# Reordering the second layer of a two-layer decoder step, with part of the state updates put off to the output projection

## The chip, the cores and the metric

The kernel runs on one core of a Trainium2 chip. The metric is the device time of one launch in microseconds (us). Before the change the median of three runs is 906.81 us (906.51 to 907.01). The profile comes from one further execution, taken by the hardware profiler.

The engines are TensorE (PE; its weight loads are shown apart, as PEld), VectorE (DVE), ScalarE (ACT), GpSimd (POOL) and SyncE (SP). SP and POOL mostly issue transfers here. Matrix results land in PSUM, which has eight banks; everything else lives in SBUF.

## The reference

One inference step of a decoder of two layers, width 2048, for 256 prompt tokens and 8 single sample tokens, 264 columns in all. Cut to what matters:

```python
# layer 0: sliding-window attention, 24 query heads; layer 1: HGRN2 recurrence, 12 heads of 128
# both: 4 memory cross-attention heads, a SiLU gate, one output projection, post-LayerNorm
q, f, iv, mq, g = _split(jnp.einsum('btd,de->bte', h, w_in), HG_SPLITS)
fg = lb + (1.0 - lb) * jax.nn.sigmoid(f)
qh, kh, vh = jax.nn.silu(q), 1.0 - fg, iv
# per token and head: state = fg * state + outer(kh, vh);  o = qh @ state
o = o * lax.rsqrt(jnp.mean(jnp.square(o), -1, keepdims=True) + RMS_EPS) * norm_w
branch = jnp.concatenate([o, mem_o], -1) * jax.nn.silu(g)
y = _layer_norm(ALPHA * h + jnp.einsum('bte,ed->btd', branch, w_out), ln_w, ln_b)
```

The memory heads of the sample tokens read cached keys and values (`cache_mem_k`, `cache_mem_v`); those of the prompt read keys and values projected from `mem_prompt`. Every sample token has its own 128x128 state for each of the 12 recurrent heads; the new states are outputs. The kernel also returns caches and the states of the prompt.

## The kernel before

**The stream.** Nearly all work hangs on one list of units, each with a block of 128 x 2048 float32 numbers (1 MB) that SP loads from memory: 16 x 128 x 128 weights of one output block, or a cache block, or states. `Stream.run` (L105) walks the list. A block passes through a `raw` buffer (four of them); ScalarE (L97) writes its high float16 half and VectorE (L98) the low half into an `hl` buffer (four of them too); then the unit's function uses it on TensorE. A raw buffer is free once its block is split, except for units added with `whole=True`: those write into the raw block and hold it until the unit is done. Splitting runs up to three units ahead of the unit that is being written.

**A projection.** `proj` (L307) multiplies the sixteen 128x128 blocks with the 264 columns of `xhl`, in three passes for each (high by high, high by low, low by high; L303 to L305), so 48 matmuls, into one of two PSUM banks with the tag `pj`. In layer 0 the keys and values of `kv_unit` take both `pj` banks and two more; in `mv_unit`, the last units before layer 1, the memory values take both `pj` banks.

**Side work.** Attention and recurrence are generators in the queue `side`. `after` (L1278) runs after each unit and moves the front generator on by one step (`pump(1)`). `hg_side` (L1064) computes one pair of recurrent heads over the prompt in ten steps; `memp_side` (L603) one memory head in two. `later` and `due` hold work that is put off by one unit, such as `hv_rows` (L1041).

**Layer 1.** For each of the six pairs the list has two forget gates (`f_unit`, L983), two value blocks (`hv_unit`, L1023), and then for each head a query block (`hq_unit`, L1009), the head's half block of states (`state_unit`, L1197) and, for heads below 8 (`NG1`), the head's gate (`early_gate`, L1051). Then come the four memory queries, with the four memory heads as side work, the four key-cache blocks (`ck_unit`, whose last one runs the softmax `mems_soft`, L659), the four value-cache blocks (`cv_unit`), with the remaining gates between and behind them, and then sixteen output units (`out_unit`, L767).

**A state unit** computes the sample tokens' outputs of one head by small matmuls (L1222 to L1226), and then updates the head's eight states in the raw block: L1233 spreads the value rows by matmuls with the selection matrix `sel`, ScalarE multiplies by the forget gate (L1237), VectorE adds the outer product (L1238), POOL writes the block out (L1241).

**Output units** add the projection to the residual stream (`residual`, L745), which frees the `pj` bank, and gather sums for the normalisation. The last eight keep their split weights in buffers of their own (`hold`) and treat first 176 columns, then, in `finish_tokens` (L841), the other 88.

**Order.** The code is traced in this order, and a planner then orders the instructions of each engine by their place in the program and by its own estimate of times. `tc.issue_after(x)` puts instructions of the same engine behind instruction `x`.

Of the kernel before, what the change touches and what calls it, by code (L numbers as in the profile page):

```python
# [18 lines left out]
P = 128  # L19
NC = 16  # L20
# [13 lines left out]
NG1 = 8  # L34
# [12 lines left out]
LEVELS = (1, 2, 4, 8, 16, 32, 64)  # L47
NMASK = (len(LEVELS) - 1) * 64

# [8 lines left out]
class Stream:  # L58


    def __init__(self, nc, pool, nraw, nsplit):
        self.nc, self.pool = nc, pool
        self.nraw, self.nsplit = nraw, nsplit
        self.units = []
        self.raw = {}
        self.hl = {}

# [37 lines left out]
    def run(self, pump):  # L105
# [11 lines left out]
        for i in range(n):  # L117
# [8 lines left out]
            while free < prepped and (free <= i or self.units[free][5]):  # L126
                free += 1
# [7 lines left out]
def trunk_kernel(  # L135
# [75 lines left out]
    bias_s = pm.tile([P, 2, NQ], F32, name="bias_s")  # L211

# [94 lines left out]
    def proj(hl, src, n, name, cols=slice(None), tag="pj"):  # L307
        w = hl.rearrange("p s (c f) -> p s c f", c=NC)
        pt = bank(tag, 2, name)
# [75 lines left out]
    def q_unit(j):  # L385
        def fn(hl):
            load_bias(j)
            load_bias(j + 1)
            pt = proj(hl, xhl, T, f"q{j}")
# [326 lines left out]

    fin = {0: deque(), 1: deque()}
# [14 lines left out]
    def silu2(out, pt):  # L732
        nc.scalar.activation(out, pt, AF.Tanh, scale=0.5 * CP)
        nc.vector.scalar_tensor_tensor(out, out, 1.0, pt, op0=ALU.add, op1=ALU.mult)
# [10 lines left out]
    def residual(l, i, cols, n, pt):  # L745
        z = xres[:, i, cols]
        summed = nc.vector.scalar_tensor_tensor(z, z, ALPHA / CP, pt, op0=ALU.mult, op1=ALU.add)  # L747
# [235 lines left out]
    def f_unit(h):  # L983
        def fn(hl):
# [4 lines left out]
            pt = proj(hl, xhl, T, f"f{h}")  # L989
            i = h % 2  # L990
            if i == 0:
# [3 lines left out]
                cur["ks8"] = p1.tile([P, 2, TS], F32, tag="ks8", name=f"ks8{h}", bufs=2)  # L995
            fg, kk, ks8 = cur["fg"][:, i], cur["kk"][:, i], cur["ks8"][:, i]
# [6 lines left out]
            nc.vector.tensor_scalar_mul(ks8, kk, 1.0 / (SA * SK))  # L1003
# [5 lines left out]
    def hq_unit(h):  # L1009
        def fn(hl):  # L1010
# [5 lines left out]
            if h % 2 == 1:  # L1016
                side.append(hg_side(h // 2, cur["q"], cur["vn"], cur["fg"], cur["qk"]))
# [3 lines left out]
    later, due = [], []  # L1021

    def hv_unit(h):  # L1023
        def fn(hl):
# [3 lines left out]
            if i == 0:  # L1028
                cur["vn"] = p1.tile([P, 2, 2, P], F32, tag="vn", name=f"vn{h}", bufs=2)
                cur["vr"] = p1.tile([P, 2, P], F16, tag="vr", name=f"vr{h}", bufs=2)  # L1030
# [10 lines left out]
    def hv_rows(h, vt, vs, vn, vr):  # L1041
# [7 lines left out]
        nc.vector.tensor_copy(vr[:, i], p16)  # L1049
# [14 lines left out]
    def hg_side(pi, q, vn, fg, qk):  # L1064
# [119 lines left out]
        for i, sq in enumerate(sqs):  # L1184
# [3 lines left out]
            scaled = mix[:, h] if h >= NG1 else sq  # L1188
# [3 lines left out]
            if h < NG1:  # L1192
# [4 lines left out]
    def state_unit(h):  # L1197
        def fn(hl):
            p1 = H["p"]
            pi, i = h // 2, h % 2  # L1200
            raw = stream.raw[state_at[h]][:, : TS * P]
            R = raw.rearrange("p (b v) -> p b v", b=TS)
            v = hl[:, :, : TS * P].rearrange("p s (b v) -> p s b v", b=TS)
            vr, fgs, ks8 = cur["vr"][:, i], cur["fg"][:, i, TP:T], cur["ks8"][:, i]
# [228 lines left out]
```

## Time and profile before

| what | value |
|---|---|
| median of three runs | 906.81 us (906.51 to 907.01) |
| profiled execution | 906.08 us |
| its span, first to last instruction | 904.3 us |
| mean granted TensorE clock | 0.994 |
| TensorE matmuls | 9281 |
| DMA | 198.67 MB, mean 220 GB/s |

Matmuls are pipelined: a row's duration covers the whole way through the array, and the next matmul may start long before it ends. A TensorE that is shown as busy is therefore not idle, and may still wait a little; idle time is counted from the end of the last matmul. The share of busy time is an average over stages. By the timeline, layer 0 ends and the first forget gate of layer 1 starts at about 420 us, the output units of layer 1 at about 800 us, and their second columns at about 878 us.

### The profile page before, as it was taken

The numbers are of one execution on the slowest core, as the hardware profiler recorded it, in microseconds if no ns is written. First come the engines' busy times: TensorE is split into PE (matmuls) and PEld (weight loads), VectorE is DVE, ScalarE is ACT, GpSimd is POOL, SyncE is SP. The second block draws the span as 40 slices with busy tenths as digits, with TensorE's granted clock in tenths as the row PEclk, the third lists the DMA queues.
The fourth block names the chain that finished last, engine by engine and source line by source line (L and its number), as shares of the span: only waits on it lengthen the run. The fifth ranks groups of instructions, "written<-read, shape, count | busy, mean of one in ns | idle before, by whom it ended". The sixth has DMA issues, their size and how long they took to land.

```text
span 904.3 us, 21814 instructions
## 1 busy us (share of the span) xinstructions
PE 886.6 (98%) x9281; PEld 762.9 (84%) x9281; DVE 701.5 (78%) x1230; ACT 582.4 (64%) x982; POOL 34.9 (4%) x68
## 2 busy tenths in 40 slices
PE   9999999999999999999999999999999999799996
PEld 6888889678888888876888888898888888688996
DVE  6879877669886666697687887979788989678736
ACT  6767776657664444476766877777777585858415
POOL 1100010000000000002000000000000000000000
PEclk9999999999999999999999999999999999899999
DMA  9998566557785555556374655827454878456303
GB/s 340 392 353 317 188 245 209 188 208 265 262 333 192 187 192 203 207 198 214 127 292 137 216 201 174 299 101 260 160 215 164 303 283 308 172 207 244 130 2 97
DMA packets 37853, 198.67 MB, mean 220 GB/s; under 512 B 4555, under 2 KB 10732, under 8 KB 17532
## 3 DMA queue, kind: packets, MB, share of 16 engines
q1 hardware_dynamic: 33024, 181.55, 56.3%
q0 software_dynamic: 4688, 15.67, 4.6%
q8 instruction: 72, 1.18, 0.5%
q14 instruction: 25, 0.20, 0.1%
q10 hardware_dynamic: 44, 0.07, 0.0%
HBM read 180.03 MB, written 17.22 MB: 218 GB/s over the span
## 4 chain that ended last, share of the span: by engine, by line
PE 77%; DVE 8%; ACT 6%; DMA 6%; issue 3%; SPq 0%; ACTq 0%; DVEq 0%
PE o L303 5%; PE o L305 5%; PE o L304 5%; PE g L305 5%; PE g L303 5%; PE g L304 5%; DVE hl L98 4%; ACT hl L97 2%; PE hv L305 2%; PE hv L303 2%; PE hv L304 2%; DMA raw<-in_w_in 2%; PE hq L303 2%; PE hq L305 2%; PE hq L304 2%
## 5 line engine op out<-in xcount | busy, mean ns | idle before, releaser
L98 DVE SCALAR_TENSOR_TENSOR hl<-raw,hl 128x2048 f16<-128x2048 f32 (+2 forms) x168 | 358.6, 2138 | 82.0 <-ACT hl L97 81.0
L97 ACT ACTIVATE hl<-raw 128x2048 f16<-128x2048 f32 (+2 forms) x168 | 299.2, 1784 | 97.8 <-PE o L305 45.4
L305 PEld LDWEIGHTS <-hl 128*128 128x128 f16 (+2 forms) x2048 | 197.4, 98 | 31.8 <-DVE hl L98 2.9
L303 PEld LDWEIGHTS <-hl 128*128 128x128 f16 (+2 forms) x2048 | 197.3, 98 | 30.6 <-issue 2.2
L304 PEld LDWEIGHTS <-hl 128*128 128x128 f16 (+2 forms) x2048 | 197.4, 98 | 30.3 <-issue 2.2
L305 PE MATMUL g<-xhl,hl 128*128 128x264 f16 x512 | 142.0, 277 | 2.4 <-DVE hl L98 2.4
L303 PE MATMUL g<-xhl,hl 128*128 128x264 f16 x512 | 141.9, 277 | 0.0
L304 PE MATMUL g<-xhl,hl 128*128 128x264 f16 x512 | 141.9, 277 | 0.0
L303 PE MATMUL o<-mix,hl 128*128 128x264 f16 x384 | 105.4, 276 | 0.8 <-DVE xres L747 0.8
L304 PE MATMUL o<-mix,hl 128*128 128x264 f16 x384 | 105.8, 276 | 0.0
L305 PE MATMUL o<-mix,hl 128*128 128x264 f16 x384 | 105.7, 276 | 0.0
L303 PE MATMUL q<-xhl,hl 128*128 128x264 f16 x192 | 53.0, 276 | 1.0 <-DVE kst L251 1.0
L303 PE MATMUL f<-xhl,hl 128*128 128x264 f16 x192 | 52.9, 276 | 0.4 <-DVE mvhl L251 0.4
L305 PE MATMUL hv<-xhl,hl 128*128 128x264 f16 x192 | 53.0, 276 | 0.0
L303 PE MATMUL hq<-xhl,hl 128*128 128x264 f16 x192 | 53.0, 276 | 0.0
L304 PE MATMUL hq<-xhl,hl 128*128 128x264 f16 x192 | 53.0, 276 | 0.0
L305 PE MATMUL hq<-xhl,hl 128*128 128x264 f16 x192 | 53.0, 276 | 0.0
L304 PE MATMUL hv<-xhl,hl 128*128 128x264 f16 x192 | 53.0, 276 | 0.0
L303 PE MATMUL hv<-xhl,hl 128*128 128x264 f16 x192 | 53.0, 276 | 0.0
L304 PE MATMUL q<-xhl,hl 128*128 128x264 f16 x192 | 53.0, 276 | 0.0
L305 PE MATMUL q<-xhl,hl 128*128 128x264 f16 x192 | 53.0, 276 | 0.0
L304 PE MATMUL f<-xhl,hl 128*128 128x264 f16 x192 | 52.9, 276 | 0.0
(338 smaller groups left out, 1858.4 us busy)
## 6 DMA issues: line engine op xcount, KB each, us to landing
raw<-in_w_in SPq DMA_DIRECT2D x88, 1024.0 KB, 6.4
raw<-in_w_o SPq DMA_DIRECT2D x32, 1024.0 KB, 5.0
raw<-in_w_mk SPq DMA_DIRECT2D x8, 1024.0 KB, 4.9
raw<-in_w_mv SPq DMA_DIRECT2D x8, 1024.0 KB, 4.9
raw<-in_c_mk SPq DMA_DIRECT2D x8, 1024.0 KB, 5.1
raw<-in_c_mv SPq DMA_DIRECT2D x8, 1024.0 KB, 7.0
raw<-in_state SPq DMA_DIRECT2D x12, 512.0 KB, 5.4
out_ss<-raw POOLq DMA_DIRECT2D x12, 512.0 KB, 5.5
```

Of the source, the lines that this page charges most:

```text
L97: hi = self.nc.scalar.activation(hl[:, 0, s], raw[:, s], AF.Copy, scale=scale)
L98: lo = self.nc.vector.scalar_tensor_tensor(hl[:, 1, s], raw[:, s], scale, hl[:, 0, s], op0=ALU.mult, op1=ALU.subtract)
L303: mm(out, lhs(0), rhs(0), start=start, stop=False)
L304: mm(out, lhs(0), rhs(1), start=False, stop=False)
L305: return mm(out, lhs(1), rhs(0), start=False, stop=stop)
```

## The change

**Order of layer 1.** The list now begins with the first forget gate and the memory queries; the eight cache blocks stand one by one between projections of the first two pairs, with `q0` and `g0` between the last key block and the first value block. Every unit says how many side steps follow it (`pumps`: 0 behind caches and states, 2 behind many projections of the recurrence). Gates of heads 0, 1, 2, 4 and 6 (`EARLY`) stand within the pairs; eleven gates stand at the end. 

**State units.** One for each pair, with the whole 1 MB block; the small operations run once on both heads.

**Updates.** Heads 0 to 5 are updated at their pair, the second head one unit later (`later`); the raw block is held one unit longer (`longer`). For heads 6 to 11 (`LATER`) the value rows, forget gates and keys are written to memory (`kept`), and their raw block is free after the split. `fetch` reads the states and what was kept again, on POOL's queue, into buffers of the memory heads that are no longer used (three homes), first behind the seventh of the last gates. `with_update` updates one head behind the residual of output units 1, 3, 5, 7, 9 and 11, and fetches the head three later.

**Banks.** The first query of layer 0 and the first forget gate of layer 1 take the bank `pv`, and do all 32 passes with the high weights before the 16 with the low ones (`apart`).

**Scaling.** The factor of `ks8` moves into `sel`.

```diff
-NG1 = 8
+EARLY = (0, 1, 2, 4, 6)
+LATER = tuple(range(6, HD))
+KEPT = P // 2 + 2 * TS
...
-            while free < prepped and (free <= i or self.units[free][5]):
+            while free < prepped and (free + self.longer.get(free, 0) <= i or self.units[free][5]):
...
+    kept = {pi: dp.tile([P, 2, KEPT], F32, name=f"kept{pi}") for pi in sorted({h // 2 for h in LATER})}
...
+        if apart:
+            pt = bank("pv", 1, name)
+            for k, (c, s, r) in enumerate([(c, 0, r) for c in range(NC) for r in range(2)] + [(c, 1, 0) for c in range(NC)]):
+                mm(pt[:, :n], w[:, s, c], src[:, r, c, cols], start=k == 0, stop=k == 3 * NC - 1)
+            return pt[:, :n]
...
-            pt = proj(hl, xhl, T, f"q{j}")
+            pt = proj(hl, xhl, T, f"q{j}", apart=j == 0)
...
-            pt = proj(hl, xhl, T, f"f{h}")
+            pt = proj(hl, xhl, T, f"f{h}", apart=h == 0)
...
-            nc.vector.tensor_scalar_mul(ks8, kk, 1.0 / (SA * SK))
...
+    def update(h, R, vr, fgs, ks, sel):
+        for g in range(2):
+            pvb = bank("pt", 2, f"vb{h}{g}")
+            for bb in range(4):
+                mm(pvb[:, bb * P : (bb + 1) * P], sel[:, 4 * g + bb], vr, start=True, stop=True)
+            for bb in range(4):
+                b = 4 * g + bb
+                s = R[:, b]
+                nc.scalar.activation(s, s, AF.Copy, scale=fgs[:, b : b + 1])
+                nc.vector.scalar_tensor_tensor(
+                    s, pvb[:, bb * P : (bb + 1) * P], ks[:, b : b + 1], s, op0=ALU.mult, op1=ALU.add
+                )
+        nc.gpsimd.dma_start(ss_o[h // 2, :, h % 2 * TS * P : (h % 2 + 1) * TS * P], R.rearrange("p b v -> p (b v)"))
...
+    def fetch(h):
+        if not homes:
+            aside["sel"] = cp.tile([P, TS, P], F16, tag="ms", name="late_sel", bufs=2)
+            nc.gpsimd.dma_start(aside["sel"], sel_d)
+            aside["kept"] = cp.tile([P, len(LATER), KEPT], F32, tag="ms", name="late_kept", bufs=2)
...
+            for t in (mkhl, mvhl, mqhl):
...
+        homes.rotate(-1)
+        aside[h] = homes[-1]
+        nc.gpsimd.dma_start(aside[h], state[h // 2][:, (h % 2) * TS * P : (h % 2 + 1) * TS * P])
...
+    def with_update(fn, k):
+        def f(hl):
+            fn(hl)
+            with tc.issue_after(marks["o"].ins):
+                late_update(LATER[k])
+                if k + 3 < len(LATER):
+                    fetch(LATER[k + 3])
...
+            if 2 * pi in LATER:
+                tail = vr[:, :, P // 2 :]
+                nc.vector.tensor_copy(tail[:, :, :TS], fgs)
+                nc.vector.tensor_copy(tail[:, :, TS:], ks)
+                nc.gpsimd.dma_start(kept[pi], vr)
+                return
...
+            half(0)
+            later.append(lambda: half(1))
...
+    f_of(0)
+    for h in range(NM):
+        w1("mq", h, mem1_sides(mq_unit(h)) if h == NM - 1 else mq_unit(h))
+    cache(c_mk, ck_unit, 0)
+    f_of(1, 2)
+    cache(c_mk, ck_unit, 1)
+    v_of(0, 2)
+    cache(c_mk, ck_unit, 2)
+    v_of(1)
+    cache(c_mk, ck_unit, 3)
+    q_of(0)
+    gate_of(0)
+    cache(c_mv, cv_unit, 0)
+    gate_of(1)
+    cache(c_mv, cv_unit, 1)
+    q_of(1)
+    cache(c_mv, cv_unit, 2)
+    f_of(2, 2)
+    cache(c_mv, cv_unit, 3)
+    f_of(3, 2)
+    state_of(0)
...
+    for k, j in enumerate([j for j in range(NC) if j not in EARLY and j not in last] + list(last)):
+        w1("g", j, fetch_first(gate_unit(1, j)) if k == 6 else gate_unit(1, j))
...
-        pump(1)
+        pump(pumps.get(i, 1))
...
-        sel[b, b] = 1
-        sel[TS + b, b] = 1
+        sel[b, b] = 1 / (SA * SK)
+        sel[TS + b, b] = 1 / (SA * SK)
```

175 lines of the change are left out of this document (101 added, 74 removed).

## The prediction

> **What bounds the kernel now.** I read the page first, then the list of waits of TensorE, then a table of stretches, then the timeline at the places where TensorE waits.
>
> ```profile
> span 904.3 us, 21814 instructions
> PE 886.6 (98%) x9281; PEld 762.9 (84%) x9281; DVE 701.5 (78%) x1230; ACT 582.4 (64%) x982; POOL 34.9 (4%) x68
> ```
>
> TensorE is busy for 98% of the span. The arithmetic stays nearly the same, so a reordering can only win back idle time of TensorE and time at a reduced clock. The idle time, by what ended it:
>
> ```profile
> PE g L305 <- DVE hl L98: 2.4, 2, 1.7
> PE hpo L1169 <- ACT st L1147: 1.5, 1, 1.5
> ...
> PE q L303 <- DVE kst L251: 1.0, 1, 1.0
> PE mback L677 <- DVE mrows L674: 1.0, 1, 1.0
> PE o L303 <- DVE xres L747: 0.8, 2, 0.5
> PE f L303 <- DVE mvhl L251: 0.4, 1, 0.4
> PE msc L303 <- ACT osq L1183: 0.4, 1, 0.4
> PE hpo L1171 <- ACT s L1162: 0.3, 1, 0.3
> ```
>
> The stretches (columns: stretch, length, busy time of each engine with its count, granted clock, share of the DMA engines, GB/s) say where this lies:
>
> ```profile
> 420.00:700.00 280.00, 279.64 (x2947) 247.47 (x2947) 229.01 (x441) 204.80 (x372) 13.09 (x24) 1.00 0.57 199
> 700.00:740.00 40.00, 39.96 (x469) 35.61 (x467) 34.63 (x67) 27.09 (x33) 1.61 (x3) 1.00 0.76 277
> 740.00:762.00 22.00, 22.00 (x274) 19.47 (x273) 22.00 (x26) 15.03 (x15) 0.00 (x0) 1.00 0.89 322
> 762.00:800.00 38.00, 32.50 (x368) 26.91 (x366) 30.70 (x51) 26.93 (x47) 0.54 (x1) 0.91 0.61 228
> 800.00:847.00 47.00, 46.23 (x416) 40.14 (x415) 37.31 (x42) 32.12 (x32) 0.00 (x0) 1.00 0.60 221
> 847.00:878.00 31.00, 31.00 (x406) 30.82 (x405) 12.43 (x30) 3.75 (x11) 0.00 (x0) 1.00 0.01 2
> ```
>
> One jam stands out, 762 to 800 us: TensorE idles 38.00 - 32.50 = 5.5 us and runs at 0.91 of its clock. From 420 to 762 it idles 0.4 us in all. Just before the jam VectorE is busy 22.00 of 22.00 us: there the last pair of recurrent heads, the four memory heads, eight cache blocks and the gates all fall together. The timelines of TensorE and ScalarE show how it closes:
>
> ```profile
> 769.24 1.91 ACT L97 ACTIVATE hl<-raw 128x2048 f16<-128x2048 f32 x1 [3.84 <-issue]
> 775.73 0.28 PE L677 MATMUL mback<-ident,mrows 32*128 32x32 f32 x2 [0.99 <-DVE mrows L674]
> 777.00 0.17 PE L696 MATMUL mso<-msphl,hl 128*128 128x2 f16 x1
> ```
>
> The value-cache blocks (mso) are split early, but cannot be multiplied before the softmax of the key scores is back (mback, 775.73). Until then they sit in the four split buffers, ScalarE has nowhere to write a gate's weights (idle 3.84 us before 769.24), and the gates come late.
>
> **The change, part by part.**
>
> *Layer 1 in another order.* Cache blocks and memory heads go to the front, one cache block to each projection, before the first recurrent side work starts; between the last key block and the first value block stand two projections (q0, g0) where one gate stood. The last stretch keeps eleven gates and the last pair. What this can win is the whole jam: 5.5 us idle, 38 x (1 - 0.91) = 3.4 us of clock, and the refill after each wait. Idle is counted from the modelled end of a matmul (0.28 us), while matmuls follow each other every 0.11 us, so six waits (g twice, hpo twice, mback, msc) cost 6 x 0.17 = 1.0 us more. Together 9.9 us.
>
> By the Trainium skill, "TensorE: Matmul & The Clock Gate", Part 1, the clock is halved only after about 3.4 us without work. Here it fell though the longest wait on the list inside the stretch is 1.7 us, so the measured 0.91 decides; by the page's rule the dip had another cause, and 3.4 us of the 9.9 would stay.
>
> Does the work fit elsewhere? Rows of 420 to 800 us, VectorE and then ScalarE:
>
> ```profile
> L98 DVE SCALAR_TENSOR_TENSOR hl<-raw,hl 128x2048 f16<-128x2048 f32 x64 | 146.6, 2292 | 21.2 <-ACT hl L97 20.8
> L1238 DVE SCALAR_TENSOR_TENSOR raw<-vb,ks,raw 128x128 f32<-128x128 f32 x96 | 26.7, 345 | 0.2 <-PE vb L1233 0.2
> L98 DVE SCALAR_TENSOR_TENSOR hl<-raw,hl 128x1024 f16<-128x1024 f32 x12 | 14.7, 1222 | 1.8 <-ACT hl L97 1.7
> L1003 DVE TENSOR_SCALAR ks<-kk 128x8 f32<-128x8 f32 x12 | 2.2, 184 | 0.1
> L1227 DVE TENSOR_REDUCE qf<-hos 128x8 f32<-128x16 f32 x12 | 2.1, 171 | 1.8 <-PE hos L1226 1.8
> L1228 DVE TENSOR_TENSOR qk<-hos,hvt 128x8 f32<-128x8 f32 x12 | 1.9, 157 | 0.0
> L1237 ACT ACTIVATE raw<-raw,fg 128x128 f32<-128x128 f32 x96 | 29.5, 391 | 3.5 <-DVE hl L98 3.5
> ```
>
> VectorE is busy 229.01 + 34.63 + 22.00 + 30.70 = 316.3 of 380 us there. It loses half of the state updates (48 x 26.7/96 = 13.4), the twelve ks8 scalings (2.2), 14.7 - 6 x 2.29 = 1.0 by splitting six state blocks instead of twelve halves, and about 6.5 by doing the seven small operations of a state unit (1.9 to 2.1 us each in sum) six times instead of twelve. Six pairs of copies (under 0.2 us each) come back. About 295 remain for 370 us, 80%. A pair without one gate unit loses its cover of 5.4 us of TensorE (48 matmuls at 0.112) but also its split, 2.29 us of VectorE; the middle stays about as full as it is, and there it hardly waits today.
>
> The put-off half lands behind the residuals of output units 1, 3, 5, 7, 9 and 11. VectorE has 78 - 37.31 - 12.43 = 28 us free between 800 and 878, ScalarE 78 - 32.12 - 3.75 = 42; the updates bring 13.4 and 48 x 29.5/96 = 14.8. They fit in sum. The danger is order: a burst of eight (2.2 us) and a split (2.29) can stand before the next residual, which frees a projection bank. Eight-unit stretch by TensorE: 48 x 0.112 = 5.4 us a unit, no wait; the later units take 31.00/406 x 48 = 3.7 us, so 2.2 + 2.3 + 0.3 = 4.8 is 1.1 too long, at most at three or four of them. Bounds 0 to 4 us; I take 1.0, since VectorE has finished its splits early in this stage today (12.43 of 31 us from 847). Ending early also clears the tail: unit 11 lies four units before the end of the stage.
>
> *Transfers.* The fetches go to POOL's queue: 3 MB of state read again, three small writes and reads of what is kept, and the twelve write-outs, of which six move.
>
> ```profile
> raw<-in_state SPq DMA_DIRECT2D x12, 512.0 KB, 5.4
> out_ss<-raw POOLq DMA_DIRECT2D x12, 512.0 KB, 5.5
> ```
>
> The DMA engines are at 0.60 from 800 to 847 and 0.01 after, which hides them; uncovered, 3 MB would be some 14 us at 221 GB/s. Head k+3 may be fetched when head k is written out: 2.2 + 5.5 + 5.5 = 13 us, against six units between them (2 x 5.4 + 4 x 3.7 = 25.6 us at worst). POOL queues nothing urgent behind these waits; SP's weight loads are not behind them. On SP, six full state loads replace twelve half ones.
>
> By the Trainium skill, "SBUF — State Buffer", section "SBUF: two separate sides", a transfer issued from GpSimd can starve while VectorE runs certain two-port operations, which speaks against moving fetches to POOL. The rows do not show it: 5.5 us there against 5.4 on SP. By the page the fetches would come late, which is a rival below.
>
> *A bank of their own.* The first query waits for a bank that the key copies still read, the first forget gate for one that the memory values still fill:
>
> ```profile
> 29.22 0.28 PE L305 MATMUL kv<-xhl,hl 128*128 128x264 f16 x1
> 30.50 0.27 PE L303 MATMUL q<-xhl,hl 128*128 128x264 f16 x1 [1.00 <-DVE kst L251]
> ...
> 419.28 0.38 PE L593 MATMUL mv<-hl,mhl 128*128 128x512 f16 x1
> 420.09 0.27 PE L303 MATMUL f<-xhl,hl 128*128 128x264 f16 x1 [0.43 <-DVE mvhl L251]
> ```
>
> Start to start is 1.28 us against 0.11, and 0.81 against 0.22: 1.17 and 0.59 us. What is late next is q0's own split:
>
> ```profile
> 25.34 1.91 ACT L97 ACTIVATE hl<-raw 128x2048 f16<-128x2048 f32 x1 [2.71 <-DMA raw<-in_w_in]
> ...
> 27.28 2.29 DVE L98 SCALAR_TENSOR_TENSOR hl<-raw,hl 128x2048 f16<-128x2048 f32 x1 [2.77 <-ACT hl L97]
> ```
>
> The high half is there at 27.25, the low half at 29.57; with the 32 high passes first the low one is needed at 29.3 + 32 x 0.112 = 32.9. Both waits go; the arrival at later weights is 1.2 us earlier, and the next units have a larger lead. I take 1.0 + 0.5 (bounds 0 and 1.76).
>
> *Fewer matmuls.* The ones-products fall from 24 to 12:
>
> ```profile
> L1226 PE MATMUL hos<-qkh,ones 128*128 128x8 f16 x24 | 2.3, 166 | 0.0
> ```
>
> Half of 2.3 us is the upper bound; each 0.166 is mostly pipeline under its neighbours, so I take 0.3.
>
> **The sum.** 9.9 + 1.0 + 0.5 + 0.3 = 11.7 us off, and on: 1.0 in the output stage, and 1.0 for new small waits in layer 1 (0 to 3; 0.4 us today over 342 us). Net 9.7. The profiled execution took 906.1 us for a span of 904.3, so it would take 896.4; the median of the runs is 906.8, 0.7 above, so about **897.0**.
>
> **Rivals.**
>
> *The jam moves to the front.* The value-cache blocks now share their stretch with the first recurrent pair and the first state unit. If their softmax is late again, the same buffers clog, and up to the 9.9 us come back: 897 to 907, half of it (902) as a value. For: VectorE needs about 35 us there (nine splits, 20.6; one update, 2.2; two thirds of a pair's side work: what the rows above leave of 316.3 us is 112, under 19 a pair, so 12) for four projections (21.6), four cache blocks and side products, about 28 us of matmuls. Against: two projections instead of one cover the softmax, and splits stand ahead of side work.
>
> *The output stage pays.* VectorE's bursts delay residuals at every later unit: 4 us instead of 1.0, 900.
>
> *The clock stays low for another reason.* The stretch 762 to 800 is granted 0.91 while the longest wait is 1.7 us; if another cause holds it, 3.4 us remain: 900.4. Against it: every other stretch up to 878 has 1.00.
>
> *POOL's transfers come late.* An update that waits for its block stands in VectorE's queue before the next residual. It decides when write and fetch take over 25.6 - 2.2 = 23.4 us; at three times the 5.5 us row (33) head 11 is 9.6 us late: 907.
>
> *State blocks starve the weights (the slower side).* In pairs 0, 1 and 2 the raw buffer is now held until the second half, issued after the following unit, is written out. Today's chain of waits already runs through such a buffer:
>
> ```profile
> 515.43 1.38 DVE raw L1238 x5
> ...
> 519.78 7.85 DMA raw<-in_w_in
> ```
>
> If the second half runs where it is written and the fourth unit behind takes that buffer: state unit and next unit with its side work about 7.8 us, update 2.2, write 5.5, load 7.9, split 1.9 + 2.3 = 27.6 us, against three projections (16.2) with side products and the state unit, an estimated 20.4 us. That is 7.2 us of waiting three times, 21.6, and the total is 919. It decides from the point where the write-out lands later than 20.4 - 12.1 = 8.3 us after the state unit starts on TensorE. Against: today updates run long before their unit,
>
> ```profile
> 512.30 0.61 PE L1233 MATMUL vb<-vr,sel_t 128*128 128x128 f16 x8
> ...
> 521.68 0.17 PE L1222 MATMUL hos<-qfh,hl 128*128 128x2 f16 x1
> ```
>
> (9 us ahead here), and the other three buffers turn over meanwhile.
>
> **How the numbers follow.** The forecast gets 0.57. The front jam gets 0.16 (0.08 faster, 0.06 within, 0.02 slower), the output stage 0.08 (faster), the clock 0.03 (faster), POOL 0.02 (slower), starving 0.14 (0.01 faster, 0.01 within, 0.12 slower). A difference of 0.2%, 1.8 us, is about what a measurement of this kernel can tell from no change. So faster 0.77, same 0.07, slower 0.16. Everything won at no cost (9.9 + 1.76 + 0.3 + the 0.8 at o) gives 894.0; a little below is the low end, 893. The upper end takes in the output stage and nearly all of the front jam: 906.
>
> **What would show it.** Right: no stretch of layer 1 with TensorE idle over 1 us in 20, clock 1.00 there, VectorE below full for every 20 us, q and f gone from the list of waits, VectorE busier by some 13 us in the output stage with TensorE's wait for xres below 2 us. Wrong: a wait of g, f or hq for hl behind a state unit (starving), mback late again near the front, or o waiting for xres at most odd units.

## The result, and the profile after

The changed kernel takes **921.66 us** (919.22 to 921.84) where the kernel before takes 906.91 us (906.51 to 907.09) in the same session: a ratio of 1.0157 [1.0139, 1.0175]. The forecast was 897.0, range 893 to 906: wrong in sign, and outside the range. The kernel before was timed again beside each group of runs below, with medians of 905.79 to 906.55 us; every ratio is to the one of its own group.

The profiled execution took 921.59 us, its span 919.8. First TensorE's waits of the changed kernel (engine, line, what it waited for: us in all, times, longest):

```profile
PE hq L307 <- DVE vs L255: 4.8, 2, 2.9
PE o L307 <- ACT mix L739: 4.8, 1, 4.8
PE o L307 <- DVE xres L757: 4.3, 3, 2.5
PE hs L307 <- ACT qk L1088: 2.2, 3, 1.2
...
PE hpo L1178 <- ACT st L1156: 1.1, 1, 1.1
PE rms L1191 <- ACT osq L1186: 0.9, 1, 0.9
```

Of the waits of before, g for hl, q for kst, f for mvhl and mback are gone; hpo still waits a little for st and s, and o for xres 4.3 us where it was 0.8. New ones took the place of the rest. The table of stretches of the same kernel says where:

```profile
660.00:720.00 60.00, 51.87 (x514) 43.75 (x513) 38.53 (x73) 41.62 (x76) 3.26 (x6) 0.97 0.47 167
720.00:797.00 77.00, 77.00 (x808) 67.88 (x807) 64.05 (x104) 50.15 (x74) 1.63 (x3) 1.00 0.49 169
797.00:822.00 25.00, 18.36 (x167) 15.12 (x166) 10.70 (x19) 11.53 (x19) 0.54 (x1) 0.86 0.24 90
822.00:850.00 28.00, 28.00 (x259) 24.48 (x257) 26.64 (x39) 21.94 (x24) 2.15 (x4) 1.00 0.78 293
850.00:887.00 37.00, 32.73 (x408) 31.56 (x406) 25.13 (x62) 13.50 (x29) 2.67 (x5) 1.00 0.36 136
```

The old jam ahead of the output stage is quite gone (77.00 of 77). TensorE now idles 8.1 us at 660 to 720, 6.6 at 797 to 822 and 4.3 at 850 to 887. In the first two of these stretches VectorE is busy 38.53 of 60 us and 10.70 of 25, and ScalarE 41.62 and 11.53: TensorE waits although no other engine is full. So each engine waits for another in turn, and the question is what order makes them do so.

For the comparisons below I worked out of each trace what TensorE lost: the time from the start of one matmul to the start of the next, less the mean of that step for the same shape without a wait in the kernel before. That counts idle time and time at a reduced clock alike. The end of TensorE's work less this loss lies between 875.9 and 876.9 us in every run here, so the loss accounts for the differences. Each row is one profiled execution, and that is its grain: ahead of 420 us all kernels but `before` and `spread4_one_bank` run the same code, and still lose between 5.4 and 10.1 us there. The profiled execution of no_put_off, at 923.44 us, was also its slowest. A difference of one or two us in one cell shows little by itself. In us, by stretch:

```
                  0-420  420-640  640-720  720-800  800-830  830-end   sum
before              7.6      1.0      0.3     10.1      0.5      1.0  20.6
after               5.9      2.9     11.9      0.1      9.4      5.1  35.3
bank_alone          6.6      0.7      0.7     11.4      0.8      0.8  21.1
no_put_off         10.1      1.9     11.4      3.4     10.4      1.1  38.3
act_behind          5.9      2.2      9.7      1.7      2.6      1.3  23.4
raised200           6.5     17.4      1.2      3.9      5.6      3.5  38.0
first2              6.6      6.5      5.2      0.8      8.7      2.0  29.8
first1              5.8     13.0      0.4      0.6      9.0      0.9  29.7
mem_last            6.7      0.4      6.5     11.1      1.3      0.6  26.4
cv_last             6.5      1.3     11.6      6.6      2.0      1.3  29.2
caches_last         7.3      0.7     10.5     12.6      0.0      0.6  31.7
own_queue           5.4      6.4      4.8      1.0      2.0      1.3  20.8
spread4             5.5      2.0      2.1      2.7      0.2      1.3  13.8
spread5             6.4      1.5      1.9     10.5      0.0      0.4  20.7
spread4_no_put      6.1      2.0      9.2      3.8      9.0      1.1  31.1
spread4_hoist       6.3      1.6      4.1      1.9      2.0      5.1  20.8
spread4_one_bank    7.5      1.5      2.1      1.6      2.0      1.3  16.1
```

After less before: 10.0 won at 720 to 800 and 1.7 ahead of 420; 1.9, 11.6, 8.9 and 4.1 lost in the others. By the sums that is 14.7 us, by the medians 14.75.

**Two things are seen in the trace of after.** The first is on ScalarE, whose timeline has these rows (start, duration, line, operation, count, idle time before and what ended it):

```profile
671.42 1.86 ACT L1214 ACTIVATE mkhl<-mkhl,late_kept 128x128 f32<-128x128 f32 x6 [4.40 <-DMA late_kept<-kept]
673.30 1.28 ACT L1192 ACT_TABLE_LOAD   x1
...
718.66 0.48 ACT L1192 ACTIVATE osq<-rms,eps_rms 128x264 f32<-128x264 f32 x1 [0.98 <-PE rms L1191]
720.23 2.15 ACT L1214 ACTIVATE mqhl<-mqhl,late_kept 128x128 f32<-128x128 f32 x7 [1.09 <-DMA late_kept<-kept]
722.29 0.46 ACT L1192 ACTIVATE osq<-rms,eps_rms 128x264 f32<-128x264 f32 x1
...
856.38 2.45 ACT L1214 ACTIVATE mvhl<-mvhl,late_kept 128x128 f32<-128x128 f32 x8 [3.56 <-DMA mvhl<-in_state]
858.74 3.69 ACT L100 ACTIVATE held<-raw 128x2048 f16<-128x2048 f32 x2
```

L1214 scales a put-off head's states. Those of heads 6 to 8, meant for the output stage, run at 671 to 678 and 720 to 724 us, in the midst of the pairs. The line that puts the update off binds VectorE only: `issue_after` holds back the instructions of the engine of the one that it names. ScalarE takes its instructions in order, so it stands 4.40 us for a transfer with the logarithm and the exponential of a pair behind it. At the second place VectorE stands 7.95 us for such an exponential, as the first row here shows:

```profile
724.52 0.49 DVE L1198 SCALAR_TENSOR_TENSOR osq<-osb,small_t,osq 128x264 f32<-128x264 f32 x1 [7.95 <-ACT osq L1195]
...
860.67 2.29 DVE L101 SCALAR_TENSOR_TENSOR held<-raw,held 128x2048 f16<-128x2048 f32 x1 [3.36 <-ACT held L100]
```

The second row is the output stage: the block of head 10, fetched late (issue to landing 10.0 us in the median of the two `mvhl<-in_state`, against 5.4 for `raw<-in_state` before), stops ScalarE for 3.56 us in front of two splits of output weights; VectorE's half of the split and the residual behind it come late, and o waits 2.5 us.

The second thing is the recurrence of the prompt. Its ten steps are one chain a pair, and a pair can hardly begin before the one ahead of it is done: st, prod and kn have one buffer each. By the timeline (us; query: a pair's last query matmul ends; hd: its chain begins):

```
             query, pairs 0 to 5           hd, pairs 0 to 5              last rms   first o
before       459 512 565 618 664 702       459 512 565 618 669 730       777        799.9
after        497 535 583 630 682 729       489 564 620 675 721 775       812        797.5
first2       452 521 577 634 681 727       452 521 609 668 719 768       810        796.1
mem_last     452 503 547 594 639 686       452 511 570 626 674 715       768        805.2
own_queue    451 514 566 622 687 723       451 514 575 628 687 748       799        798.8
spread4      451 516 569 626 672 716       451 516 575 627 690 741       792        791.8
```

Before, the chain began with the queries until the last two pairs. A chain needs both heads of its pair, and those of pair 0 now stand apart: their hd start at 489 and 501 us, where before they started at 459 and 463. So the chain goes on 38 us later. The pairs follow each other in 38 to 52 us while the chain takes 46 to 63 a pair (hd to hd, pair 0 counted from 501): it is 29 to 46 us behind from the second pair on, and ends when the output units already run. ScalarE's timeline of after shows how that reaches TensorE:

```profile
660.82 0.38 ACT L1171 ACTIVATE s<-pu 128x256 f32<-128x256 f32 x1 [3.21 <-PE pu L1167]
...
662.05 1.91 ACT L100 ACTIVATE hl<-raw 128x2048 f16<-128x2048 f32 x1 [0.57 <-PE hv L309]
663.87 0.58 ACT L1182 ACTIVATE osb<-hpo 128x512 f32<-128x512 f32 x1
...
665.87 0.18 ACT L253 ACTIVATE vs<-hv 128x8 f16<-128x8 f32 x1
```

ScalarE stands 3.21 us for a chain's pu; the copy of vs, which must read the value bank before hq may have it, stands behind that chain's work until 665.87. TensorE's hq waits 2.9 us for it.

### The profile page after: what moved, and what is told of

The parts are those of the page before. It is cut to its first block, busy times and chain, and to the rows that moved or that the text cites. A ratio compares the mean times of both kernels' runs of the same rounds, so it can differ in the third digit from the quotient of the medians.

```text
span 919.8 us, 21726 instructions
## 1 busy us (share of the span) xinstructions
PE 889.2 (97%) x9269; PEld 762.6 (83%) x9269; DVE 694.2 (75%) x1176; ACT 581.3 (63%) x964; POOL 42.1 (5%) x81
## 4 chain that ended last, share of the span: by engine, by line
PE 68%; issue 21%; ACT 4%; DVE 3%; DMA 2%; POOL 1%; ACTq 0%; POOLq 0%; DVEq 0%
PE g L307 6%; PE g L308 6%; PE g L309 6%; PE o L307 5%; PE o L308 5%; PE o L309 5%; PE q L307 2%; PE q L309 2%; PE q L308 2%; PE mk L307 2%; PE mk L308 2%; PE mk L309 2%; PE mv L600 2%; PE mv L602 2%; PE mv L601 2%
## 5 line engine op out<-in xcount | busy, mean ns | idle before, releaser
L307 PEld LDWEIGHTS <-hl 128*128 128x128 f16 (+2 forms) x2016 | 194.5, 98 | 35.0 <-issue 7.2
L308 PEld LDWEIGHTS <-hl 128*128 128x128 f16 (+2 forms) x2016 | 194.7, 98 | 34.2 <-issue 6.1
L309 PEld LDWEIGHTS <-hl 128*128 128x128 f16 (+2 forms) x2016 | 194.6, 98 | 28.6 <-issue 0.2
L307 PE MATMUL hq<-xhl,hl 128*128 128x264 f16 x192 | 53.8, 280 | 4.9 <-DVE vs L255 4.8
L309 PE MATMUL hq<-xhl,hl 128*128 128x264 f16 x192 | 53.8, 280 | 0.0
L308 PE MATMUL hq<-xhl,hl 128*128 128x264 f16 x192 | 53.7, 280 | 0.0
L307 PE MATMUL o<-mix,held 128*128 128x176 f16 (+1 forms) x256 | 44.5, 222 | 4.3 <-DVE xres L757 4.3
L307 PE MATMUL q<-xhl,hl 128*128 128x264 f16 x176 | 48.6, 276 | 0.0
L308 PE MATMUL q<-xhl,hl 128*128 128x264 f16 x176 | 48.6, 276 | 0.0
L309 PE MATMUL q<-xhl,hl 128*128 128x264 f16 x176 | 48.6, 276 | 0.0
L309 PE MATMUL f<-xhl,hl 128*128 128x264 f16 x176 | 48.6, 276 | 0.0
## 6 DMA issues: line engine op xcount, KB each, us to landing
l_d<-l_t POOLq DMA_DIRECT2D x4, 861.0 KB, 12.6
```

The lines of the kernel that those rows point to most:

```text
L307: mm(out, lhs(0), rhs(0), start=start, stop=False)
L308: mm(out, lhs(0), rhs(1), start=False, stop=False)
L309: return mm(out, lhs(1), rhs(0), start=False, stop=stop)
```

## The experiments

### The bank alone

The kernel before with only the bank of their own for q0 and f0.

```diff
-            pt = proj(hl, xhl, T, f"q{j}")
+            pt = proj(hl, xhl, T, f"q{j}", apart=j == 0)
...
-            pt = proj(hl, xhl, T, f"f{h}")
+            pt = proj(hl, xhl, T, f"f{h}", apart=h == 0)
```

> The kernel before with one part of the change alone: the first query and the first forget gate in the bank pv, high halves first. By every theory the two waits (1.17 and 0.59 us start to start) go and nothing else moves: about 905.3 us against 906.9, q and f gone from the list of waits. If the time is 906.9 still, the won time is lost again further down, and the part is worth nothing.

906.52 us, ratio 0.9993 [0.9979, 1.0008]. Both waits are gone, and no gain is measured, though the interval still holds the 1.5 us expected. In the one profile the last query of the pairs ends 1.3 us earlier than before (700.7 for 702.0), and the first o begins at 799.9 as before. The loss at 720 to 800 is 1.3 us larger, with a new wait (the first row) in the old jam:

```profile
PE mpo L303 <- ACT mphl L249: 1.7, 1, 1.7
PE hpo L1174 <- ACT st L1152: 1.5, 1, 1.5
```

So in this execution what came earlier to the jam waited longer in it.

### Nothing put off

The changed kernel with all updates in their state units.

```diff
-LATER = tuple(range(6, HD))
+LATER = ()
```

> The changed kernel with no update put off (LATER empty): all twelve heads are updated at their pair, nothing is kept or fetched again. Theory of the chain (each pair's recurrent side work is one serial chain, it starts 42 us later in the new order and falls about one pair behind, until double-buffered tiles run out at 660 to 720 us and the output projection waits for the last pair at 811): the lag and the wait of the output stay, 914 to 922 us. Theory of the put-off updates (their scalings and fetches stand in ScalarE's queue ahead of the chain, and their bursts delay residuals): nearly all of the loss goes, 898 to 904 us, with no wait over 1 us.

919.8 us, ratio 1.0147 [1.0111, 1.0182]. The output stage no longer waits for xres, but the loss at 640 to 720 and the wait of o for mix (4.8 us) stand as in after. So the late chain does not come of putting off; the new order of layer 1, with its state units merged, costs 13 us without it. (The wait of hq for vs is not on this list; others stand in its place.)

### The scalings bound on ScalarE too

```diff
-        squared = nc.scalar.activation(sq[:, :n], z, AF.Square)
+        squared = marks["sq"] = nc.scalar.activation(sq[:, :n], z, AF.Square)
...
-            with tc.issue_after(marks["o"].ins):
+            with tc.issue_after(marks["o"].ins), tc.issue_after(marks["sq"].ins):
```

> The changed kernel with ScalarE's scalings of the put-off updates also bound behind the residual's square, where only VectorE's part was bound. Theory of the chain: the 16 scalings at 671 us leave, worth 2 to 5 us, but the last pair still ends after the output has begun: 915 to 920 us with a wait of o for mix of 2 us or more. Theory of the put-off updates: 10 us or more come back, 905 to 911 us, and the wait of o for mix is gone.

909.08 us, ratio 1.0026 [1.001, 1.0043]: 12.6 us come back. The rows of L1214 in this kernel (count, shortest, median and longest ns, from when to when):

```profile
L1214 ACT ACTIVATE mkhl<-mkhl,late_kept x16: 384/387/389, 819.2 to 855.6; 128x128 f32<-128x128 f32 x16
L1214 ACT ACTIVATE mvhl<-mvhl,late_kept x16: 384/385/388, 830.1 to 861.5; 128x128 f32<-128x128 f32 x16
```

All of them are in the output stage now. By the table of losses 6.8 us were won at 800 to 830 (the last rms ends at 806 instead of 812) and 3.8 behind; only 2.2 at 640 to 720, where hq still waits 2.9 us. o still waits 2.2 us for mix: the time is the one that the theory of the put-off updates gave, and the wait is the one that the theory of the chain gave, so both faults are there. With the scalings bound, putting off is worth 10.7 us against the run before this one.

### Side work ahead of all else

The changed kernel, its side steps in layer 1 planned with a raised priority.

```diff
-                    next(side[0])
+                    with tc.high_priority(200) if lift else nullcontext():
+                        next(side[0])
```

> The changed kernel with the side work of layer 1 raised by 200 places in the planner's priority, so that it stands ahead of splits of later blocks. Theory of the chain: the lag of the pairs falls below 20 us, the waits of hq for vs and of o for mix go, 900 to 909 us; the waits for xres in the output stage (4.3 us) may stay. Theory of the put-off updates: 917 us or more, since their scalings and fetches stay where they are.

923.5 us, ratio 1.0185 [1.0159, 1.0212]. The loss leaves 640 to 720 (1.2 us) and appears at 420 to 640 (17.4): now projections wait, f 2.9 us in all for its split weights among them. The lag of the pairs does fall, to 12 to 19 us, as the theory of the chain foresaw, but the chain still ends at 812. Priority moves the wait; it makes no room.

### The chain begun early

The next four hold the scalings bound and change the order of layer 1. In `first2` pair 0 comes first, and the memory head is spread over pairs 0 to 3:

```diff
-    f_of(0)
-    for h in range(NM):
-        w1("mq", h, mem1_sides(mq_unit(h)) if h == NM - 1 else mq_unit(h))
-    cache(c_mk, ck_unit, 0)
...
+    f_of(0)
+    f_of(1)
+    v_of(0)
+    v_of(1)
+    q_of(0)
+    q_of(1)
+    gate_of(0, 2)
+    mq_of(0, 2)
+    state_of(0)
...
```

> The changed kernel with the scalings bound behind the square on ScalarE (the run that gave 909.08), and layer 1's units in another order: the first pair's gates, values and queries now come ahead of the memory head's queries and caches, which are spread between pairs 1 to 3; the put-off updates stay. Chain theory: the recurrence is one serial chain of some 53 us a pair that starts 42 us later in the changed kernel than before (hd at 501 for 459) and so ends at 805 to 817, in the output stage; started at about 455 it ends near 775 and the waits of o at 800 (2.7 us) and most of those at 660 to 720 (11.5 us) go: 896 to 903 us. Rival, density: the waits come of ScalarE and VectorE being full whatever the order, so the same waits show up elsewhere: 906 to 913 us.

916.31 us, ratio 1.0109 [1.0079, 1.014]: the chain theory fell as it stood. The chain began at 452 and yet ended at 810. Pair 1's took 88 us (521 to 609): its last rms ended at 585, and then the memory head's eight side steps, which stood in the same queue, had their turn from 587 on. `first1` has the memory's queries and caches as a block between pairs 0, 1 and 2:

```diff
+    gate_of(0)
+    state_of(0)
+    mq_of(0, 2)
+    mq_of(1, 2)
+    gate_of(1, 2)
+    mq_of(2, 2)
+    mq_of(3, 2)
+    cache(c_mk, ck_unit, 0)
+    f_of(2, 2)
...
```

> The same order as in the run before it, with the updates put off and the scalings bound behind the square on ScalarE. Chain theory: as with the other early order, 896 to 903 us; hd of the first pair near 455 and the last rms ahead of 790. Rival, density: 906 to 913 us. Against the run without putting off it gives what putting off is worth once the chain is early: by the prediction's term up to 10 us, by the rival that putting off only undoes the late chain, nothing.

916.23 us, ratio 1.0103 [1.0076, 1.013], the same miss: hd of pairs 0 and 1 at 452 and 535, 83 us apart, last rms at 810, 13.0 us lost at 420 to 640. The same order without putting off:

> Nothing put off (as in the run that gave 919.8), and layer 1's units in an order in which the first pair comes ahead of the memory head, whose queries and caches stand as a block between pairs 0, 1 and 2. Chain theory: the 13 us by which the kernel without putting off is slower than before come from the chain's late start, so they go: 903 to 910 us, and o no longer waits 4.8 us for the gated head at 820. Rival, density: the order does not matter, 915 to 922 us.

928.6 us, ratio 1.0228 [1.0195, 1.0261], a miss as well; but putting off is worth 12.4 us here too. With the memory head last, as before:

> Updates put off, scalings bound behind the square on ScalarE, and the kernel before's order of layer 1: six pairs one after another, then the memory head between the late output gates. The first hd is back at about 459. If only the chain's start counts: 896 to 903 us. If what counts is that a pair's projections (some 45 us without their updates and gates) come faster than its chain runs (some 53 us), the chain falls behind again pair by pair, the pairs' double buffers run out at 600 to 700, and the waits of hq stay though the output stage waits for nothing: 903 to 910 us.

911.24 us, ratio 1.0054 [1.0031, 1.0077]. The chain ends at 768 and the first output unit waits for nothing much (1.3 us at 800 to 830). Instead 6.5 us go at 640 to 720 (the pairs outrun the chain, the second condition of the expectation) and 11.1 at 720 to 800: the old jam, still there although half of the updates have left it.

### More units behind the last pair

With the scalings bound and the memory's queries in front as in after, the caches move behind the last pair: four of them,

```diff
     for k, j in enumerate([j for j in range(NC) if j not in EARLY and j not in last] + list(last)):
+        if k + 4 < 8:
+            cache(*caches[k + 4])
         w1("g", j, fetch_first(gate_unit(1, j)) if k == 6 else gate_unit(1, j))
```

> The run that gave 909.08 (updates put off, scalings bound behind the square on ScalarE), with one move: the four memory value caches stand between the late output gates, behind the last pair, and no longer in front of it. Tail theory: in every order so far the last pair's rms ends 75 to 92 us behind its last query, whenever the first pair began (452 to 501), so the output stage waits when fewer than some 82 us of other units lie between that query and the first o; the 11 gates and the last state unit are about 70 us, four caches more make some 82 to 85: o waits 0 to 1 us for mix (2.2 in that run) and the time is 904 to 908 us. Rival, relocation: the pairs come closer together by the caches, the waits of hq for vs at 660 to 720 (11.5 us of excess) grow by what is won at 800: 908 to 913 us.

915.16 us, ratio 1.0087 [1.0063, 1.011], or all eight (`k` in place of `k + 4`):

> As the run beside it, with all eight memory caches behind the last pair; the memory head's queries and its side work stay in front. Tail theory: no wait for mix at the first o, as there. Against the order with the whole memory head last (911.24, with 10.3 us of excess at 740 to 780) it tells whether that jam is of the memory's side work, which here is done by 500: then the tail has under 3 us of excess and the time is 902 to 907 us. Rival, relocation: the pairs, 13 us shorter in sum, run further ahead of their chain and hq waits more at 620 to 720: 908 to 914 us.

917.01 us, ratio 1.0104 [1.0079, 1.013]. In cv_last o waits 1.6 us for mix, in caches_last no more, where 12.6 us are lost at 720 to 800 with all the memory's side work done by 500. So the memory's side steps aren't needed for a jam in that stretch; caches, gates and the last pair's chain are enough. The tail theory was wrong on both times. Relocation was nearer, but both times lie above its ranges too, and most of what came back did so at 720 to 800 (6.6 and 12.6 us, against 1.7 in act_behind) and not in the waits of hq that it named: 11.6 and 10.5 at 640 to 720, against 9.7.

### A queue of their own for the memory's steps

`own_queue` puts pair 0 first and the memory's queries into pairs 1 to 3. Their side steps stand in a second queue and are taken two to four a pair; the key caches follow pair 3, the value caches stand between the late gates.

```diff
+    def mem_of(h):
+        def fn(hl):
+            mq_unit(h)(hl)
+            beside.append(memp_side(1, h))
...
         pump(pumps.get(i, 1))
+        if i in beside_at:
+            while beside and next(beside[0], 0) == 0:
+                beside.popleft()
```

> Updates put off, scalings bound behind the square. The first pair comes first; the memory head's queries are spread over pairs 1 to 3, its side steps stand in a queue of their own instead of in the one queue of side work and are taken two to four a pair in pairs 2 to 4, its key caches follow pair 3, its value caches stand between the late gates. Queue theory: the recurrence fell behind in the orders that began at 452 because the eight memory steps stood in its queue (one pair took 83 to 88 us there, some 53 elsewhere) and because a pair with 45 us of projections is shorter than its chain; here each pair has 50 to 55 us of units and no memory step ahead of it, so hd follows hq within 10 us up to pair 4, the last rms ends ahead of 790, hq waits under 2 us, and the time is 895 to 902 us, faster than before. Rival, density: VectorE and ScalarE are the limit from 460 to 800, the chain still loses 5 to 10 us a pair, and the time is 906 to 914 us.

908.64 us, ratio 1.0023 [1.001, 1.0037]. Most of the mechanism came out, the time did not. hd follows the query within 9 us up to pair 4 and no hq waits; the last rms ends at 799, not ahead of 790. But 9.5 us are lost at 580 to 660 (by the same reckoning, in finer steps), in the stretch of the four key caches in a row, where VectorE is busy 16.43 and then 18.81 of 20 us and the clock is reduced:

```profile
620.00:640.00 20.00, 17.32 (x257) 14.76 (x255) 16.43 (x39) 17.55 (x29) 0.55 (x2) 0.88 0.39 139
640.00:660.00 20.00, 18.77 (x186) 14.92 (x186) 18.81 (x21) 13.49 (x17) 0.24 (x1) 0.78 0.87 315
```

### The key caches parted

`spread4` has one memory query in each of pairs 0 to 3, two memory steps in each of pairs 1 to 4, and the key caches between the projections of pair 4.

```diff
+        keys = pi == 4
         f_of(2 * pi, 2)
+        if keys:
+            cache(c_mk, ck_unit, 0)
+        if 1 <= pi <= 4:
+            aside_next()
+        f_of(2 * pi + 1, 2)
+        if keys:
+            cache(c_mk, ck_unit, 1)
...
```

> The order of the run with a queue of its own for the memory steps (908.64), with the four key caches parted between the projections of pair 4, where they stood in a row behind pair 3, and one memory query in each of pairs 0 to 3. If the row of four caches made the 9.1 us of excess at 620 to 660 (their splits ahead of the next projection's on VectorE), that falls under 2 us and nothing takes its place: 899 to 903 us, faster than before by 0.4 to 0.8%. Rival, relocation (VectorE and ScalarE have no room for the second layer's work whatever the order): the excess comes back at 660 to 740, 905 to 909 us.

**901.67 us** (900.0 to 903.48), ratio **0.9949 [0.9937, 0.9962]**: faster than before by 0.5%. Against own_queue three things moved (the queries, the memory steps and the caches), so the 7.0 us between the two aren't shown to be the caches' alone. Its waits and one stretch:

```profile
PE o L307 <- ACT mix L739: 1.6, 1, 1.6
...
PE hs L308 <- DVE qk L1089: 1.0, 1, 1.0
PE hs L307 <- ACT qk L1088: 0.8, 2, 0.6
PE o L307 <- DVE xres L757: 0.7, 1, 0.7
```

```profile
660.00:720.00 60.00, 58.89 (x633) 51.34 (x631) 49.00 (x81) 40.19 (x63) 3.24 (x6) 1.00 0.63 232
```

TensorE is busy 58.89 of 60 us where it was busy 51.87 in after, and VectorE does 49.00 us of work there where it did 38.53. With the key caches in pair 5 instead (`keys = pi == 5`):

> As the run beside it, with the key caches between the projections of pair 5. The last pair's projections are longer by the four caches, so its recurrence starts less far behind its query (25 us in the run with the row of caches, about 6 here by the order), but there is less behind it to hide its end: the last rms at 785 to 800. If the row was the cause: 898 to 903 us; by relocation 905 to 909 us, with o waiting over 2 us for mix at the first o.

907.04 us, ratio 1.0017 [1.0005, 1.003]: the same caches one pair later lose 10.5 us at 720 to 800, where the value caches and the gates follow at once. The chain is on time (last rms at 791) and o waits for no mix, against the second expectation, so this loss is not the late chain. The order of spread4 with nothing put off:

> The first of these orders with nothing put off: all six pairs' updates in their state units. If the prediction's term was right and only the order hid it, putting off is worth some 8 to 11 us and this takes 908 to 914 us. If putting off only undid the late chain, which this order does without it, it takes within 2 us of the run with the updates put off.

916.79 us, ratio 1.0129 [1.0111, 1.0147]. By the medians putting off is worth **15.1 us** in this order, more than the 8 to 11 expected. It is not won where the forecast looked for it: of the difference in the table 1.1 us lie at 720 to 800, but 7.1 at 640 to 720 and 8.8 at 800 to 830. Without putting off the chain is late in this order too (the last rms ends at 814 and o waits 4.8 us for mix, against 792 and 1.6), so the expectation's "which this order does without it" was wrong. With the updates put off again, spread4 with the scalings let go on ScalarE:

```diff
-            with tc.issue_after(marks["o"].ins), tc.issue_after(marks["sq"].ins):
+            with tc.issue_after(marks["o"].ins):
```

> The kernel that gave 901.67, with the scalings bound behind the residual on VectorE alone, as in the changed kernel. If their place on ScalarE is a fault of its own, worth about what it was there (12.6 us): 911 to 916 us, with ScalarE standing for late_kept or a fetched block ahead of work of the pairs, and waits of o for xres of 2 us and more in the output stage. If it hurt only because the chain was late: 901 to 904 us.

907.97 us, ratio 1.002 [1.0006, 1.0035]: 6.3 us, half of what it was beside the late chain; neither expectation had that size. The wait of o for xres is as the first one foresaw:

```profile
PE o L307 <- DVE xres L757: 4.2, 3, 2.2
```

Last, q0 and f0 back in the common banks (`apart` left out of both calls):

> The same kernel with q0 and f0 back in the common pair of banks, low halves in their turn. By the prediction's terms (1.0 us for q0, 0.5 us for f0) 902.9 to 903.4 us, with q waiting 1.0 us for kst at 29 and f 0.4 us for mvhl at 419. If the later stages take it up, as in the kernel before: within 0.5 us of 901.67.

902.42 us, ratio 0.9953 [0.9939, 0.9967]. The medians differ by 0.75 us, from two groups of runs, and the intervals overlap: whether the part is worth nothing or the 1.5 us of the forecast is not settled.

## Why the prediction was wrong

**The term of the jam was right in size.** Of 9.9 us to be won ahead of the output stage 10.0 were won (10.1 to 0.1 in the table), and the stretch of 77 us has no idle time. How much of that is the new order's merit stays open, since 11.6 us were lost just ahead of the stretch, which relieves it: spread4, which loses 2.1 us there, loses 2.7 at 720 to 800, and spread5, with 1.9, loses 10.5. The rivals that kept the jam at the front and the one of the clock did not come: 720 to 797 has 1.00, and the clock fell behind the new waits instead (0.97 at 660 to 720, 0.86 at 797 to 822). In the rival of the front jam a sum is off: the rows leave 122 us of 316.3, not 112, which makes its 12 us some 14 and changes nothing here.

**"1.0 for new small waits in layer 1 (0 to 3)" is the step that failed**, by its mechanism: 13.5 us were lost at 420 to 720 beyond before (1.9 and 11.6). I summed VectorE's work, found 295 us for 370, and called that room. At 660 to 720 VectorE did stand idle for a third of the time. The sum says nothing of a chain that runs through three engines, one pair at a time, 46 to 63 us a pair. The change moved its start by 38 us and shortened the time between pairs, and the forecast never laid the chain's end (777 before, against 799.9 for the first o: 23 us to spare) beside that. no_put_off shows that the order, with the state units merged, does this without any update put off (13 us), and own_queue and spread4 that the chain comes back beside the queries up to pair 3 when the memory's steps leave its queue. That its late start alone was the cause fell: first1, first2 and mem_last began it at 452 and were slower than before.

**The 1.0 us (0 to 4) in the output stage failed as well: order was looked for on VectorE alone.** The term was made of VectorE's bursts. The stage lost 13.0 us at 800 and behind. 10.6 of these are won back by binding the scalings on ScalarE; what is left, 3.9 against 1.5 before, lies within the bounds given. The diff has `marks["o"]` as the only anchor, and L1214 is an instruction of another engine: reading that a wait named in the source binds one queue would have shown it.

**Late transfers** were priced as a wait of VectorE from 23.4 us on; the fetch of head 10 stopped ScalarE long before that, with the splits of the output weights behind it. In act_behind the same fetches take 8.0 us (`mvhl<-in_state`), and o waits 0.7 us for xres: there the time of the transfer did no harm, since its first user no longer stood in ScalarE's queue ahead of urgent work. **State blocks** starved nothing: no wait for hl is left on the list of after.

**q0 and f0.** The waits went, as foreseen; of the 1.5 us nothing could be measured in the kernel before, where in the one profile the jam took it. The working said that the next units have a larger lead, and did not ask where that lead ends. The term of 0.3 us for fewer ones-matmuls was not tried by itself.

By the table the forecast of 897.0 would need a loss of about 11; spread4 stands at 13.8. In each of the three orders that were run with and without it, putting the updates off pays (10.7, 12.4 and 15.1 us) once the scalings are bound; in the changed kernel, where they are not, it pays nothing (921.66 against 919.8). So the order and the one engine left unbound hid it. In the order of the kernel before it was not tried both ways; mem_last comes nearest, with the updates put off, and is slower than before by 0.5%.

## What to carry to other kernels

Before you move work, lay out every serial chain that crosses engines: when it starts, how long it takes a turn, how often a turn comes, and how much lies between its end and its first user; free time summed per engine cannot show that it is late. When an operation is put off, bind each engine that takes part, since an instruction that waits for a transfer at the head of an engine's queue stops what stands behind it (ScalarE for 4.40 us here). A gain ahead of a jam can be lost in it, and a fault in one place can hide a gain of the same size in another: so measure the parts of a change both alone and in the company in which they are to run.

## What the runs showed of the hardware

TensorE's clock fell after shorter waits than I had assumed. In before the granted clock is 0.50 from 778.1 to 781.6 us and again from 785.0 to 788.4, with 1.00 between; the longest wait ahead of the first is 1.53 us, ahead of the second 1.73. Matmuls of 264 columns, 112 to 113 ns apart at full clock, stand 220 ns apart in the second of these. In own_queue the clock is 0.50 from 635.1 to 648.7 us, with waits of 0.9, 1.3, 0.3, 0.5 and 0.5 us between 631 and 645. In after it is 0.50 from 666.8 to 670.2 us, behind the wait of 2.9 us, and from 813.6 to 820.4, which begins within the wait of 4.8 us. A wait of 1.6 us in spread4 and one of 2.2 us in spread4_hoist left it at 1.00. So the length of a single wait does not decide; what does stays open. Each time at 0.50 lasted 3.4 us or a whole multiple of it (6.8 and 13.6 us above).

The Trainium skill, "TensorE: Matmul & The Clock Gate", Part 1, has the clock halve after an idle window of about 3.4 us; the step of 220 for 112 ns agrees with a half, the length of the waits does not. At 0.50 a matmul of 264 columns costs 0.11 us more: 1.3 us for 12 steps in after and 2.3 us for 21 in own_queue, on top of the wait.
